# Three of eight wide weight splits in part two of the seven-product blocks done as two single splits

## The chip, the cores and the metric

The kernel runs on one core of one Trainium2 chip. The metric is the device time of one launch in microseconds (us), the median over runs. Matrix products run on TensorE (PE), elementwise work on VectorE (DVE) and ScalarE (ACT), some DMAs and a few operations on GpSimd (POOL), and most DMAs are issued from SyncE (SP).

## The reference, cut to what matters

One decoder layer over 512 tokens of width 2048: a norm, one wide input projection, two token mixers, and an output projection that is merged with gates.

```python
u = _rmsnorm(h, norm_w)
proj = jnp.matmul(u, w_in.astype(jnp.float32))
...
h_a = _mlstm_chunkwise(...)          # 8 heads
h_b = _gated_delta_chunkwise(...)    # 16 heads
y_a = jnp.matmul(h_a, w_out[:ML_WIDTH])
y_b = jnp.matmul(h_b, w_out[ML_WIDTH:])
return jax.nn.sigmoid(gate_a) * y_a + jax.nn.sigmoid(gate_b) * y_b
```

All of it is float32. The change concerns only how the weights of the large products are prepared.

## The kernel before, in words

**Products in three pieces.** A float32 product is made from three products of reduced-precision operands: each operand x becomes a pair, hi (a rounded copy) and lo (x minus hi), and the kernel adds hi·hi, hi·lo and lo·hi. For a weight tile, hi is a cast on ACT (`split_hi`, line 140) and lo a subtraction on DVE (`split_lo`, line 143) that has to wait for the cast. In the seven-product stages the three matmuls are lines 577, 578 and 579; line 578 is the one that reads lo.

**Seven products.** Most of the input projection and part of the output projection are done in blocks that save one of eight products of 2x2 sub-matrices: `seven_stage`, called once for the 13 blocks of `SEVEN` (kinds z, z, z, z, s, s, q, v, v, g, g, g, g) and once for the 2 blocks of `OUTS` (kind y). The function `seven` runs one block. A block has two parts, A and B, and each part has eight *quads*, here called A0 to A7 and B0 to B7. A quad loads three 128x512 weight pieces (`load_quad`, line 505) and makes weight pairs from them:

- A quad of part A makes two sums (lines 519 and 520), splits one sum and one raw piece singly, and splits the other two sums, `t13`, as one 128x1024 pair. It makes four products.
- A quad of part B makes one difference `ts` (line 537, from a raw piece and a piece that part A wrote to DRAM), splits it singly, and splits its other two raw pieces as one 128x1024 pair. It makes three products, the pair's two first and that of `ts` last.

Each product is made for two halves of the tokens, three matmuls a half, so that a quad of part B issues 18 matmuls.

**Buffers.** Single splits go into the tags `wh` and `wl` of the pool `wp`, with four buffers each. Wide splits go into `w2h` and `w2l`, with two buffers each. The raw pieces lie in `wr3` with three buffers.

**Between the parts.** When the last quad of part A is done, the eight PSUM banks hold sums that part B adds to. So as each half of a product of A7 ends, the bank is added into the SBUF tile X: `copy1` (line 562, ACT) twice for the first product, and `add` (line 631, DVE) six times, in the order m1, m1, m5, m5, m7, m7. The products of B0 write m1, m5 and m7 again, each in two halves, and each half has to wait until its bank's add has read it. The last of the six adds therefore stands ahead of the sixth group of three matmuls of B0.

**What sets the order.** `prep_sums` and `prep_pair` prepare quad n+1 while quad n is multiplied. TensorE keeps the order in which the code is written. On all other engines a scheduler sets the order when the kernel is built, by priorities (`tc.high_priority`) and its own estimate of when operands are ready; on the chip each engine then goes through its list in that order.

The lines that the change touches are in `prep_pair`:

Of the kernel before, what the change touches and what calls it, by code (L numbers as in the profile page):

```python
# [30 lines left out]
KH = KT // 2  # L31
# [27 lines left out]
def hybrid_body(  # L59
# [79 lines left out]
    def split_hi(hi, src):  # L139
        newest["A"] = A.copy(hi, src).ins  # L140

    def split_lo(lo, src, hi):
        newest["V"] = V.tensor_tensor(out=lo, in0=src, in1=hi.bitcast(F32), op=ALU.subtract).ins  # L143
# [336 lines left out]
    def seven_stage(sbp, su, s4, X, t2_d, w_, k0, blocks, sinks, hook, queue):  # L480
# [4 lines left out]
        quads = [(kind, c1, c2, b, g, i) for b, (kind, c1, c2) in enumerate(blocks)  # L485
                 for g in "AB" for i in range(KH)]
# [20 lines left out]
        def split(src, wide):  # L507
            if wide:
                hi, lo = (sbp.tile([P, 2, NO], F32R, tag=f"w2{n}", name=f"w{n}", bufs=2) for n in "hl")
            else:  # L510
                hi, lo = (wp.tile([P, 1, NO], F32R, tag=f"w{n}", name=f"w{n}", bufs=NSPL) for n in "hl")
            split_hi(hi, src)
            split_lo(lo, src, hi)
            return [(hi[:, n, :], lo[:, n, :]) for n in range(2 if wide else 1)]
# [25 lines left out]
        def prep_pair(q):  # L540
            if q < len(quads):
                p_, pair = partq[q]
                with tc.high_priority(offset=2 * PRIO):
                    w2 = split(pair, True)
                partq[q] = p_ + w2 if quads[q][4] == "A" else w2 + p_

        JW, OO = ((psj, "pj"), (psw, "wk")), ((pso, "o"),) * 2
# [16 lines left out]
        def seven(n0, kind, c1, c2):  # L564
# [20 lines left out]
            for n in range(N - 2):  # L585
                prep_sums(n0 + n + 1)
                prep_pair(n0 + n + 1)
                load_quad()
                for m in range(4 if n < KH else 3):
                    if n == N - 3 and m == 2:  # L590
                        prep_sums(n0 + N - 1)
                        prep_pair(n0 + N - 1)
                    product(n, m)
# [3 lines left out]
            for n, m in ((N - 2, 0), (N - 2, 1), (N - 1, 0), (N - 1, 1), (N - 2, 2), (N - 1, 2)):  # L597
                if (n, m) == (N - 2, 1):
                    prep_sums(n0 + N)
                if (n, m) == (N - 1, 0):  # L600
                    prep_pair(n0 + N)
                    load_quad()
                if last and (n, m) == (N - 1, 1):
                    hook()
                product(n, m)
# [1159 lines left out]
```

## Time and profile before

| | us |
|---|---|
| median of 3 runs | 2178.43 (2174.1 to 2181.12) |
| the profiled execution | 2172.99 |
| its span, first to last instruction | 2171.2 |
| PE busy | 2131.3 |
| DVE busy | 1715.0 |
| ACT busy | 1035.5 |
| granted TensorE clock, mean | 0.999 |

The profile lists a matmul of 512 columns with about 0.39 us, but the next one starts 0.23 us after it: matmuls overlap in the array, so a pause of PE shows as idle time only from 0.16 us on. DVE and ACT overlap likewise at their ends by about 0.09 us. Of the 13 blocks of `SEVEN` the first starts at about 124 us and the last ends at about 1130 us; the 2 blocks of `OUTS` lie between about 1957 and 2118 us.

### The profile page before, as it was taken

What the parts mean: (1) busy time and instruction counts of PE and PEld (TensorE: products, weight loads), DVE (VectorE), ACT (ScalarE), POOL (GpSimd) and SP (SyncE); (2) the same over time, 40 slices, a digit from 0 to 9 for tenths busy, and PEclk for the clock granted to TensorE, in tenths of its full rate; (3) what the DMA queues carried; (4) which work ended last, traced back from release to release, by engine and by line L of the source; (5) the groups of instructions that cost most, each with busy time, mean ns of one, the idle gap of its engine ahead of it and who ended that gap; (6) DMA issues with size and microseconds to landing.
All of it is one profiled execution on the core that took longest, in us unless ns stands there. A gap on an engine that the chain in (4) does not pass through costs nothing. (4 is left out here: it accounts for less than half of the span.)

```text
span 2171.2 us, 31926 instructions
## 1 busy us (share of the span) xinstructions
PE 2131.3 (98%) x10544; PEld 1756.0 (81%) x10544; DVE 1715.0 (79%) x2973; ACT 1035.5 (48%) x1994; POOL 432.0 (20%) x651
## 2 busy tenths in 40 slices
PE   6999999999999999999999999999999999999998
PEld 5888888888788887878878888888888888887786
DVE  5887788788788778777866887887887878668877
ACT  5444444444444444444445546456455464435345
POOL 0000000000004000000003335234243263243211
PEclk9999999999999999999999999999999999999999
DMA  5456676667668766766766767677686677778886
GB/s 160 124 185 202 195 213 199 213 199 226 198 222 245 242 191 219 242 186 222 257 197 172 196 173 184 169 181 185 178 222 171 165 185 209 198 239 266 232 281 242
DMA packets 447143, 444.20 MB, mean 205 GB/s; under 512 B 197121, under 2 KB 303842, under 8 KB 446850
## 3 DMA queue, kind: packets, MB, share of 16 engines
q1 hardware_dynamic: 377618, 337.22, 54.1%
q0 software_dynamic: 24752, 72.90, 10.8%
q10 hardware_dynamic: 44608, 32.06, 4.6%
q8 instruction: 82, 1.34, 0.3%
q14 instruction: 83, 0.68, 0.1%
HBM read 348.66 MB, written 97.58 MB: 206 GB/s over the span
## 5 line engine op out<-in xcount | busy, mean ns | idle before, releaser
L140 ACT CAST wh<-wr 128x512 fp32r<-128x512 f32 (+1 forms) x522 | 373.2, 717 | 415.4 <-PE pj L258 231.4
L143 DVE TENSOR_TENSOR wl<-wr,wh 128x512 fp32r<-128x512 f32 (+1 forms) x522 | 437.4, 840 | 109.3 <-ACT wh L140 103.7
L257 PE MATMUL pj<-uh,wh 128*128 128x512 f32 x896 | 376.0, 420 | 0.0
L259 PE MATMUL pj<-uh,wl 128*128 128x512 f32 x896 | 350.8, 391 | 0.0
L258 PE MATMUL pj<-ul,wh 128*128 128x512 f32 x896 | 350.2, 391 | 0.0
L578 PE MATMUL ps<-wl,uh 128*128 128x512 f32 x752 | 295.0, 392 | 4.8 <-DVE wl L143 4.8
L577 PE MATMUL ps<-wh,uh 128*128 128x512 f32 x752 | 294.5, 392 | 4.1 <-DVE X L631 3.5
L579 PE MATMUL ps<-wh,ul 128*128 128x512 f32 x752 | 292.8, 389 | 0.0
L140 ACT CAST wh<-ts 128x512 fp32r<-128x512 f32 x240 | 148.2, 617 | 250.9 <-DVE ts L537 197.8
L140 ACT CAST wh<-t 128x1024 fp32r<-128x1024 f32 x120 | 126.4, 1054 | 275.7 <-PE ps L579 165.7
L577 PE MATMUL ps<-wh,suh 128*128 128x512 f32 x624 | 242.9, 389 | 1.5 <-ACT to L642 1.5
L533 POOL DMA_DIRECT2D t_d<-ts x104 | 56.6, 544 | 936.9 <-DVE ts L520 883.0
L578 PE MATMUL ps<-wl,suh 128*128 128x512 f32 x624 | 242.8, 389 | 0.0
L579 PE MATMUL ps<-wh,sul 128*128 128x512 f32 x624 | 242.7, 389 | 0.0
L259 PEld LDWEIGHTS pj<-uh,wl 128*128 128x128 f32 x896 | 168.3, 188 | 37.3
L257 PEld LDWEIGHTS pj<-uh,wh 128*128 128x128 f32 x896 | 169.0, 189 | 30.0
L258 PEld LDWEIGHTS pj<-ul,wh 128*128 128x128 f32 x896 | 169.2, 189 | 28.1
L143 DVE TENSOR_TENSOR wl<-ts,wh 128x512 fp32r<-128x512 f32 x240 | 163.7, 685 | 35.2 <-ACT wh L140 35.2
L143 DVE TENSOR_TENSOR wl<-t,wh 128x1024 fp32r<-128x1024 f32 x120 | 146.8, 1224 | 55.9 <-ACT wh L140 55.0
L578 PEld LDWEIGHTS ps<-wl,uh 128*128 128x128 f32 x752 | 141.1, 188 | 40.7 <-DVE wl L143 12.7
L577 PEld LDWEIGHTS ps<-wh,uh 128*128 128x128 f32 x752 | 141.1, 188 | 40.1 <-DVE X L631 10.8
L537 DVE TENSOR_TENSOR ts<-wr 128x512 f32<-128x512 f32 x120 | 82.8, 690 | 104.2 <-DMA wr<-t_d 86.1
(334 smaller groups left out, 3826.2 us busy)
## 6 DMA issues: line engine op xcount, KB each, us to landing
wr<-in_w_in_dram SPq DMA_DIRECT2D x744, 256.0 KB, 3.8
wr<-in_w_out_dram SPq DMA_DIRECT2D x138, 256.0 KB, 5.0
t_d<-ts POOLq DMA_DIRECT2D x104, 256.0 KB, 3.9
wr<-t_d SPq DMA_DIRECT2D x104, 256.0 KB, 3.9
xt<-in_x_dram SPq DMA_DIRECT2D x8, 512.0 KB, 7.1
tg_d<-X ACTq DMA_DIRECT2D x16, 256.0 KB, 6.9
tg_d<-to ACTq DMA_DIRECT2D x16, 256.0 KB, 6.0
v<-v_d SPq DMA_DIRECT2D x8, 512.0 KB, 5.8
```

The source lines that it names most:

```text
L140: newest["A"] = A.copy(hi, src).ins
L143: newest["V"] = V.tensor_tensor(out=lo, in0=src, in1=hi.bitcast(F32), op=ALU.subtract).ins
L257: T.matmul(ps[j], hi[:, k, wsl], uh[:, kt, :], start=(kt == 0), stop=False)
L258: T.matmul(ps[j], hi[:, k, wsl], ul[:, kt, :], start=False, stop=False)
L259: T.matmul(ps[j], lo[:, k, wsl], uh[:, kt, :], start=False, stop=(kt == KT - 1))
L533: queue.dma_start(t2_d[b % 2, i], ts[:, 0, :])
L537: V.tensor_tensor(out=ts[:, 0, :], in0=r[:, 0, :], in1=r[:, 2, :], op=ALU.subtract)
L577: T.matmul(ps[t], ah, hi, start=(g == "A" and i == 0), stop=False, skip_group_check=True)
L578: T.matmul(ps[t], ah, lo, start=False, stop=False, skip_group_check=True)
L579: T.matmul(ps[t], al, hi, start=False, stop=(i == KH - 1), skip_group_check=True)
```

## The change

In part B, the quads B1, B3 and B5 (i odd and below 7) no longer split their pair of raw pieces into one 128x1024 buffer of `w2h` and one of `w2l`, but each piece by itself into a 128x512 buffer of `wh` and of `wl`. B0, B2, B4, B6 and B7, and all of part A, stay as they were. Three quads in each of 15 blocks are touched: 45 wide casts and 45 wide subtractions become 90 and 90 of half the size. Products, their order on TensorE and all values stay the same.

```diff
         def prep_pair(q):
             if q < len(quads):
                 p_, pair = partq[q]
+                _, _, _, _, g, i = quads[q]
                 with tc.high_priority(offset=2 * PRIO):
-                    w2 = split(pair, True)
+                    if g == "B" and i % 2 and i < KH - 1:
+                        w2 = split(pair[:, 0:1, :], False) + split(pair[:, 1:2, :], False)
+                    else:
+                        w2 = split(pair, True)
                 partq[q] = p_ + w2 if quads[q][4] == "A" else w2 + p_
```

The new lines move what stands below them by four: line 577 becomes 581, line 578 becomes 582, line 631 becomes 635, line 562 becomes 566.

The scheduler also orders the work around them anew. On DVE at the passage from part A to part B of the seventh block (kind q), before; `wr_5422` holds the raw pieces of B0, `wr_5467` of B1, `wr_5505` of B2, `wr_5551` of B3, `wr_5583` of B4:

```order
L143 TENSOR_TENSOR wl<-wr_5422,wh 128x1024
L631 TENSOR_TENSOR X<-X,ps 128x512
L537 TENSOR_TENSOR ts<-wr_5505 128x512
L631 TENSOR_TENSOR X<-X,ps 128x512 x3
L143 TENSOR_TENSOR wl<-ts,wh 128x512
L631 TENSOR_TENSOR X<-X,ps 128x512 x2
L537 TENSOR_TENSOR ts<-wr_5551 128x512
L143 TENSOR_TENSOR wl<-wr_5467,wh 128x1024
L143 TENSOR_TENSOR wl<-wr_5505,wh 128x1024
L143 TENSOR_TENSOR wl<-ts,wh 128x512
L537 TENSOR_TENSOR ts<-wr_5583 128x512
```

And now, where the pieces of B0 to B4 are `wr_5494`, `wr_5539`, `wr_5577`, `wr_5627` and `wr_5659`:

```order
L143 TENSOR_TENSOR wl<-wr_5494,wh 128x1024
L635 TENSOR_TENSOR X<-X,ps 128x512
L537 TENSOR_TENSOR ts<-wr_5577 128x512
L143 TENSOR_TENSOR wl<-wr_5539,wh 128x512
L635 TENSOR_TENSOR X<-X,ps 128x512 x2
L143 TENSOR_TENSOR wl<-wr_5539,wh 128x512
L635 TENSOR_TENSOR X<-X,ps 128x512 x2
L537 TENSOR_TENSOR ts<-wr_5627 128x512
L143 TENSOR_TENSOR wl<-wr_5577,wh 128x1024
L635 TENSOR_TENSOR X<-X,ps 128x512
L537 TENSOR_TENSOR ts<-wr_5659 128x512
```

The lo halves of B1 have moved ahead of adds, as two single ones, and the last add now stands behind the difference of B3 and the wide lo half of B2. In the other blocks the rows differ a little, but in every one the last add has come to stand behind the wide lo half of B2.

On ACT at the same place, before:

```order
L140 CAST wh<-wr_5422 128x1024
L562 COPY X<-ps 128x512 x2
L140 CAST wh<-ts 128x512
L140 CAST wh<-wr_5467 128x1024
L140 CAST wh<-wr_5505 128x1024
L140 CAST wh<-ts 128x512
L140 CAST wh<-wr_5551 128x1024
L140 CAST wh<-ts 128x512 x2
L140 CAST wh<-wr_5583 128x1024
```

And now:

```order
L140 CAST wh<-wr_5494 128x1024
L566 COPY X<-ps 128x512 x2
L140 CAST wh<-wr_5539 128x512 x2
L140 CAST wh<-wr_5577 128x1024
L140 CAST wh<-wr_5659 128x1024
L140 CAST wh<-ts 128x512 x2
L140 CAST wh<-wr_5627 128x512 x2
L140 CAST wh<-wr_5727 128x1024
L140 CAST wh<-ts 128x512 x2
```

The casts of B1's pieces now come right behind the two copies, the wide cast of B4 has moved ahead of the casts of two differences, and B3's two pieces come behind those. On TensorE no row has moved. On SP one load of a mixer's values and two loads of the output projection stand a few places elsewhere in the whole program, and on POOL one load has changed places with its neighbours.

## The prediction, before the run

> **What bounds the kernel now.** First the page: how full is each engine, and what ends the pauses of the fullest.
>
> ```profile
> span 2171.2 us, 31926 instructions
> PE 2131.3 (98%) x10544; PEld 1756.0 (81%) x10544; DVE 1715.0 (79%) x2973; ACT 1035.5 (48%) x1994; POOL 432.0 (20%) x651
> ```
>
> PE lacks 40 us to the span, so whatever the change saves on DVE or ACT is worth nothing unless PE waits for it, and all that it can take off is among PE's pauses. The view of waits lists them for PE: us in total, times, the longest.
>
> ```profile
> PE pprm L108 <- POOL rs L304: 14.6, 1, 14.6
> PE ps L578 <- DVE wl L143: 5.2, 12, 0.9
> PE ps L577 <- DVE X L631: 3.5, 6, 1.4
> ```
>
> 14.6 us are the start. In the 15 blocks PE waits 12 times for a lo half, 5.2 us, and 6 times for an add into X, 3.5 us. Since a pause shows only beyond 0.16 us (0.39 us of a matmul less its spacing of 0.23), the true losses are 12 x 0.16 = 1.9 and 6 x 0.16 = 1.0 us larger. The first kind is what the change aims at.
>
> The place is the passage from part A to part B. PE in the seventh block, in order of time; 632.24 is the first matmul of B0, and a matmul follows each 0.23 us:
>
> ```profile
> 632.24 0.39 PE L577 MATMUL ps<-wh,uh 128*128 128x512 f32 x1
> ...
> 636.19 0.39 PE L577 MATMUL ps<-wh,uh 128*128 128x512 f32 x1
> ...
> 636.88 0.39 PE L577 MATMUL ps<-wh,uh 128*128 128x512 f32 x1
> 637.73 0.50 PE L578 MATMUL ps<-wl,uh 128*128 128x512 f32 x1 [0.45 <-DVE wl L143]
> ```
>
> 636.19 is the last half of B0's third product, which needs the sixth add. 636.88 is B1's first matmul. The second, which reads lo, comes 0.85 us after it, 0.62 late. DVE at the same time:
>
> ```profile
> 628.10 1.22 DVE L143 TENSOR_TENSOR wl<-wr,wh 128x1024 fp32r<-128x1024 f32 x1
> 629.24 0.68 DVE L631 TENSOR_TENSOR X<-X,ps 128x512 f32<-128x512 f32 x1
> 631.65 0.69 DVE L537 TENSOR_TENSOR ts<-wr 128x512 f32<-128x512 f32 x1 [1.73 <-DMA wr<-t_d]
> 632.26 1.88 DVE L631 TENSOR_TENSOR X<-X,ps 128x512 f32<-128x512 f32 x3
> 634.05 0.69 DVE L143 TENSOR_TENSOR wl<-ts,wh 128x512 fp32r<-128x512 f32 x1
> 634.65 1.28 DVE L631 TENSOR_TENSOR X<-X,ps 128x512 f32<-128x512 f32 x2
> 635.85 0.69 DVE L537 TENSOR_TENSOR ts<-wr 128x512 f32<-128x512 f32 x1
> 636.45 2.35 DVE L143 TENSOR_TENSOR wl<-wr,wh 128x1024 fp32r<-128x1024 f32 x2
> ```
>
> DVE runs without a gap from 631.65 on: it is the bound here, because B2's difference stood in its list ahead of five adds and waited 1.73 us for its transfer. Spacings are read here too: 0.60 us from one 512-wide operation to the next (632.26 to 634.05 for three), and 2.35 - 1.22 = 1.13 us from one wide one to the next. B1's wide lo ended at 636.45 + 1.22 = 637.67, and PE went on 0.06 later.
>
> **The change part by part.** *B1's lo halves.* Two single ones now stand ahead of adds, so the wait at B1 goes: 0.62 us in this block. *The sixth add.* In the new list it stands behind two halves of B1, B3's difference and B2's wide lo; before, only one half of a difference stood there. DVE takes its list in order: at 631.65 B2's difference sat waiting while the adds behind it did not start. So I walk the new list from that row with the spacings above: difference of B2 631.65, half 632.26, adds two and three 632.86 and 633.46, half 634.06, adds four and five 634.66 and 635.26, difference of B3 635.86, wide lo of B2 636.47, sixth add 637.60 to 638.28. PE's last half of the third product then starts at 638.34 instead of 636.19, 2.15 us later. What was waited for at B1 comes back (0.62): this block loses **1.53 us**.
>
> Do the two halves get their casts in time? ACT there:
>
> ```profile
> 627.97 1.07 ACT L562 COPY X<-ps 128x512 f32<-128x512 f32 x2
> 632.43 0.62 ACT L140 CAST wh<-ts 128x512 fp32r<-128x512 f32 x1 [3.40 <-DVE ts L537]
> 632.96 1.05 ACT L140 CAST wh<-wr 128x1024 fp32r<-128x1024 f32 x1
> ```
>
> ACT idles 3.40 us after the copies, and two casts of 0.62 fit before 632.26. The wide cast at 632.96 was B1's, in the buffer that A7 had left; that buffer now falls to B2, whose cast can end at about 634, well before 636.47.
>
> The block is not special. The ninth block had no wait at B1 and no late transfer to speak of:
>
> ```profile
> 782.90 0.68 DVE L631 TENSOR_TENSOR X<-X,ps 128x512 f32<-128x512 f32 x1
> 783.96 0.69 DVE L537 TENSOR_TENSOR ts<-wr 128x512 f32<-128x512 f32 x1 [0.38 <-DMA wr<-t_d]
> ...
> 789.31 0.39 PE L577 MATMUL ps<-wh,uh 128*128 128x512 f32 x1
> ...
> 789.99 0.39 PE L577 MATMUL ps<-wh,uh 128*128 128x512 f32 x1
> 790.22 0.39 PE L578 MATMUL ps<-wl,uh 128*128 128x512 f32 x1
> ```
>
> The same walk from 783.96 (5.95 us to the start of the sixth add) has it at 789.91 to 790.59 and PE at 790.65 instead of 789.31: a loss of **1.34**, and nothing to get back. In the second block, as in the next three, B3's difference stood ahead of the sixth add already, and waited for its transfer:
>
> ```profile
> 247.44 0.69 DVE L537 TENSOR_TENSOR ts<-wr 128x512 f32<-128x512 f32 x1 [0.31 <-DMA wr<-t_d]
> 248.05 0.68 DVE L631 TENSOR_TENSOR X<-X,ps 128x512 f32<-128x512 f32 x1
> 248.79 0.51 PE L577 MATMUL ps<-wh,uh 128*128 128x512 f32 x1 [0.54 <-DVE X L631]
> 249.60 0.40 PE L577 MATMUL ps<-wh,uh 128*128 128x512 f32 x1
> 249.92 0.51 PE L578 MATMUL ps<-wl,uh 128*128 128x512 f32 x1
> ```
>
> 248.05 is the sixth add. Now the fifth takes its place, the wide lo follows at 248.65, the sixth add runs from 249.78 to 250.46, and PE starts at 250.52 instead of 248.79: 1.73 later, less 0.1 for B1's lo, which came 0.32 after its predecessor: **1.6**. The three walks give 1.3 to 1.6; over 15 blocks at 1.5 that is **+22 us**.
>
> *Later quads.* B4 and B6 no longer share two wide buffers with B1, B3 and B5, so their casts can start earlier. The lo waits that are not at B1 can go: between nothing and the whole 5.2 + 1.9 us of the view of waits. Part of it lies at B1 and is in the walks already, so I take less than half, **-3 us**.
>
> *More instructions.* 45 wide casts and subtractions become 90 and 90 single ones.
>
> ```profile
> L143 DVE TENSOR_TENSOR wl<-wr,wh 128x512 fp32r<-128x512 f32 x402 | 291.7, 726 | 91.8 <-ACT wh L140 86.2 <-PE put L313 2.2 <-DMA wr<-in_w_out_dram 1.2
> L143 DVE TENSOR_TENSOR wl<-wr,wh 128x1024 fp32r<-128x1024 f32 x120 | 145.9, 1222 | 17.6 <-ACT wh L140 17.5
> L140 ACT CAST wh<-wr 128x512 fp32r<-128x512 f32 x402 | 247.4, 617 | 325.2 <-PE pj L258 231.4 <-PE py L1389 41.0 <-issue 13.5
> L140 ACT CAST wh<-wr 128x1024 fp32r<-128x1024 f32 x120 | 126.0, 1051 | 90.2 <-PE ps L579 71.5 <-issue 13.6 <-ACT wh L140 4.9
> 589.00:666.00 77.00, 76.48 (x336) 62.40 (x335) 64.16 (x83) 34.09 (x51) 7.68 (x14) 1.00 0.68 216
> ```
>
> By busy time ACT gains 45 x (2 x 0.617 - 1.051) = 8.2 us and DVE 45 x (2 x 0.726 - 1.222) = 10 us; by spacing, which counts in a queue without gaps, DVE gains 45 x (2 x 0.60 - 1.13) = 3.2 us. In the last row (a stretch of one block; PE, weight loads, DVE, ACT busy) DVE has 13 us to spare and ACT 43, so outside the passage I count them at nothing; without that cover they cost those 3 to 10 us. In the passage the walk has them already.
>
> [...]
>
> *Moved transfers.* One load of a mixer's values, two of the output projection (SP) and one on POOL move by a few places, each of 256 KB to 512 KB.
>
> ```profile
> wr<-in_w_out_dram SPq DMA_DIRECT2D x138, 256.0 KB, 5.0
> ```
>
> They are issued several transfers ahead; I take zero, and bound it by one landing each, 4 x 5 = 20 us at worst, nothing at best. B4's pieces can be loaded earlier, since B1's are read sooner.
>
> The sum: 22 - 3 = +19 us on the profiled execution's 2172.99 us gives 2192. The median of the runs shown is 5.4 us above that execution, which would give 2197. I put the prediction between: **2195 us**.
>
> **The rivals.** *No change (2178 us).* The sixth add cannot start earlier than its list allows: in the ninth block B0 began at 789.31 - 15 x 0.227 = 785.91, the first add 3.01 us before it, and from there to the sixth nine operations and the first take 0.60 + 5.95 us, so it ends 4.2 us after B0's first matmul, and PE needs it at 3.40. Even without any wait for a transfer a block loses 0.9 us, 13 in all; set against that everything PE waited before (5.2 + 3.5 + 2.9 = 11.6 us), the change comes out even. It needs the transfers of B2 to be on time in all blocks, and nothing in the change moves them: in the row of 631.65 the wait was 1.73 us.
>
> *Faster (2171 us).* It is decided by one point: whether the sixth add ends within 3.40 us of B0's first matmul. If it does (it would, were B2's wide lo, 1.13 us, behind it), the waits for lo halves go and nothing takes their place: -7 us. For it speaks that B1's lo is indeed ready early; against it, the list, and three walks with 1.3 us and more beyond that point.
>
> *Slower still (2210 us).* B3's and B5's halves need single buffers that the products of B1 and B3 hold, and their casts stand behind those of two differences in ACT's list. If each of these two quads waits 0.5 us for its lo half, that is 15 x 2 x 0.5 = 15 us more. A quad lasts 18 x 0.23 = 4.1 us and a cast with its lo 1.3, so the slack is there unless a transfer is late; the page's wait for `t_d` shows that some are.
>
> *The clock falls (2257 us).* If the longer pauses made the throttle grant half speed for one quad per block, 15 x 4.1 = 62 us would come on top. The longest pause in these stages says no:
>
> ```profile
> 821.75 0.39 PE L579 MATMUL ps<-wh,sul 128*128 128x512 f32 x1
> 823.59 0.50 PE L577 MATMUL ps<-wh,suh 128*128 128x512 f32 x1 [1.45 <-ACT to L642]
> 823.93 0.40 PE L578 MATMUL ps<-wl,suh 128*128 128x512 f32 x1
> 824.16 0.39 PE L579 MATMUL ps<-wh,sul 128*128 128x512 f32 x1
> ```
>
> After 1.84 us between two starts the spacing is back at 0.23 with the third matmul. [...]
>
> **How the numbers follow.** About 0.3% (6.5 us) is what a measurement of this kernel can tell from no change. Forecast, the late sixth add: 0.75, 2195 us, by itself 2187 to 2203. Slower still: 0.10. The clock: 0.01. No change: 0.09. Faster: 0.05. So slower by over 0.3%: 0.85 (0.01 of the forecast's chance falls within the bound instead), within: 0.10, faster: 0.05. The range reaches from 2184, into the no-change case, to 2207, into the slower one; outside lie faster, most of no change and half of slower still, not quite 0.2.
>
> **What would show it.** In the new profile: PE's waits for an add into X grow from 3.5 to 20 us or more, at the third product of B0, and those for a lo half shrink below 2 us. DVE's rows at the passage have the sixth add behind a 128x1024 lo. PE's busy time stays within some us of 2131 while the span grows. If PE waits at B3 or B5 instead, the third rival holds; if the sixth add is in time, the walk's spacings were wrong.

## The result and the profile after

| | before | after |
|---|---|---|
| median of 6 runs, us | 2180.66 (2174.1 to 2184.57) | 2193.91 (2192.01 to 2197.74) |
| ratio, 95% interval | | 1.0065 [1.0047, 1.0083] |
| profiled execution, us | 2172.99 | 2193.82 |
| its span, us | 2171.2 | 2192.1 |

The change makes the kernel slower by 0.65%, 13 us by the medians and 21 by the two profiled executions; that of before lay 7.7 us under its median, that of after at its median. What before's slower executions wait for is only in part on record (its second profile, below). The page of after, span and busy times:

```profile
span 2192.1 us, 31988 instructions
PE 2134.5 (97%) x10544; PEld 1756.7 (80%) x10544; DVE 1711.6 (78%) x3018; ACT 1047.3 (48%) x2039; POOL 431.2 (20%) x651
```

No engine has become the bound: PE is busy 3 us longer in a span that is 21 us longer, DVE 3 us less although it has 45 instructions more. What grew is PE's waiting. The view of waits for PE (us in total, times, the longest):

```profile
PE ps L581 <- DVE X L635: 22.3, 29, 1.3
PE pprm L108 <- POOL rs L304: 15.2, 1, 15.2
PE ps L582 <- DVE wl L143: 5.0, 5, 3.0
```

The wait for an add into X was 3.5 us in 6 times and is 22.3 in 29. That for a lo half has hardly changed in sum (5.2 to 5.0), but comes 5 times in place of 12.

The passage of the seventh block, first DVE from the first add to the sixth, then PE from B0's first matmul to the sixth group:

```profile
637.53 0.68 DVE L635 TENSOR_TENSOR X<-X,ps 128x512 f32<-128x512 f32 x1
639.66 0.69 DVE L537 TENSOR_TENSOR ts<-wr 128x512 f32<-128x512 f32 x1 [1.45 <-DMA wr<-t_d]
640.27 0.68 DVE L143 TENSOR_TENSOR wl<-wr,wh 128x512 fp32r<-128x512 f32 x1
640.87 1.28 DVE L635 TENSOR_TENSOR X<-X,ps 128x512 f32<-128x512 f32 x2
642.07 0.69 DVE L143 TENSOR_TENSOR wl<-wr,wh 128x512 fp32r<-128x512 f32 x1
642.67 1.28 DVE L635 TENSOR_TENSOR X<-X,ps 128x512 f32<-128x512 f32 x2
643.86 0.69 DVE L537 TENSOR_TENSOR ts<-wr 128x512 f32<-128x512 f32 x1
644.47 1.22 DVE L143 TENSOR_TENSOR wl<-wr,wh 128x1024 fp32r<-128x1024 f32 x1
645.60 0.68 DVE L635 TENSOR_TENSOR X<-X,ps 128x512 f32<-128x512 f32 x1
```

```profile
640.54 0.39 PE L581 MATMUL ps<-wh,uh 128*128 128x512 f32 x1
...
644.66 0.39 PE L583 MATMUL ps<-wh,ul 128*128 128x512 f32 x1
646.34 0.50 PE L581 MATMUL ps<-wh,uh 128*128 128x512 f32 x1 [1.28 <-DVE X L635]
```

The sixth add starts 5.94 us after B2's difference; the walk in the prediction had 5.95. It ends at 646.28, and PE's sixth group starts at 646.34. Without a pause matmuls of 512 columns follow one another at 0.227 us (before, 700.19 to 711.98: 52 spacings in 11.79 us), so that group would start 15 x 0.227 = 3.40 us after B0's first matmul; it starts 5.80 after it, against 3.95 before. There is no pause any more at B1.

One sum serves all kernels below. For each product matmul of the 15 blocks I take from the trace its start less that of the one before it less 0.227 us, and add up what is over 0.015 us: **at the passage** (the 18 matmuls of B0 and the first 4 of B1) and **elsewhere**. Before has 14.5 and 8.1 us, after 33.5 and 9.8: 20.7 more, and the span is 20.9 longer. So the whole loss between these two executions is in these pauses, 19.0 us of it at the passage. There the sixth group of three matmuls has 20.0 us against 2.4 before, the five groups ahead of it 13.5 against 6.4 (the adds two to five have the halves of B1 ahead of them), and B1 nothing against 5.8.

### The profile page after: what moved, and what is told of

It reads as the page before. It is cut to its first block, busy times and chain, and to the rows that moved or that the text cites. A ratio compares the mean times of both kernels' runs of the same rounds, so it can differ in the third digit from the quotient of the medians.

```text
span 2192.1 us, 31988 instructions
## 1 busy us (share of the span) xinstructions
PE 2134.5 (97%) x10544; PEld 1756.7 (80%) x10544; DVE 1711.6 (78%) x3018; ACT 1047.3 (48%) x2039; POOL 431.2 (20%) x651
## 3 DMA queue, kind: packets, MB, share of 16 engines
q8 instruction: 82, 1.34, 0.3%
## 5 line engine op out<-in xcount | busy, mean ns | idle before, releaser
L140 ACT CAST wh<-wr 128x512 fp32r<-128x512 f32 (+1 forms) x567 | 381.9, 676 | 552.4 <-PE pj L258 237.8
L143 DVE TENSOR_TENSOR wl<-wr,wh 128x512 fp32r<-128x512 f32 (+1 forms) x567 | 442.6, 783 | 109.8 <-ACT wh L140 104.7
L581 PE MATMUL ps<-wh,uh 128*128 128x512 f32 x752 | 296.5, 394 | 20.5 <-DVE X L635 20.1
L582 PE MATMUL ps<-wl,uh 128*128 128x512 f32 x752 | 294.0, 391 | 4.5 <-DVE wl L143 4.5
L583 PE MATMUL ps<-wh,ul 128*128 128x512 f32 x752 | 293.5, 390 | 0.0
L582 PE MATMUL ps<-wl,suh 128*128 128x512 f32 x624 | 242.8, 389 | 0.0
L583 PE MATMUL ps<-wh,sul 128*128 128x512 f32 x624 | 242.7, 389 | 0.0
L582 PEld LDWEIGHTS ps<-wl,uh 128*128 128x128 f32 x752 | 141.5, 188 | 34.0 <-DVE wl L143 5.7
```

The source lines that it names most:

```text
L581: T.matmul(ps[t], ah, hi, start=(g == "A" and i == 0), stop=False, skip_group_check=True)
L582: T.matmul(ps[t], ah, lo, start=False, stop=False, skip_group_check=True)
L583: T.matmul(ps[t], al, hi, start=False, stop=(i == KH - 1), skip_group_check=True)
```

## The experiments

`issue_after(i)` tells the scheduler to put an instruction behind `i`; both are on DVE here, and the moved row follows at the usual spacing (below, the wide lo 0.60 us after the add, at 637.25 and 636.65). All kernels but the last two in this table were timed in 5 rounds beside runs of before; a second profile of after and of before is in brackets.

| kernel | median, us | ratio to before, 95% | span | at the passage | elsewhere |
|---|---|---|---|---|---|
| only B1 split | 2194.39 | 1.0061 [1.0044, 1.0078] | 2193.7 | 39.4 | 3.8 |
| only B3 and B5 split | 2176.11 | 0.9976 [0.9964, 0.9987] | 2178.7 | 15.7 | 12.3 |
| not split in kind y | 2192.90 | 1.0051 [1.0036, 1.0067] | 2190.5 | 31.3 | 9.6 |
| B2's wide lo behind the sixth add | 2172.11 | 0.9958 [0.9944, 0.9972] | 2171.4 | 20.5 | 2.6 |
| and B3's difference | 2169.11 | 0.9961 [0.9945, 0.9976] | 2165.3 | 13.3 | 3.8 |
| and B2's difference | 2157.49 | 0.9903 [0.9888, 0.9919] | 2156.4 | 2.0 | 6.0 |
| the same, only B3 and B5 split | 2163.26 | 0.9927 [0.9912, 0.9942] | 2157.9 | 3.6 | 5.1 |
| before, B2's difference behind the sixth add | 2168.21 | 0.9952 [0.9934, 0.9970] | 2165.5 | 6.4 | 11.0 |
| after (again) | 2193.91 | 1.0065 [1.0047, 1.0083] | 2192.1 (2195.1) | 33.5 (36.7) | 9.8 (9.8) |
| before (again) | 2180.66 | | 2171.2 (2176.0) | 14.5 (15.5) | 8.1 (10.4) |

The kernel with the best median has only four runs. In all twelve profiles the span less the two sums lies between 2148.1 and 2150.7 us, whatever was split and in whatever order. That is the strongest reading of the study: to within 2.6 us no other part of the program gained or lost.

### Which of the three quads carries the loss

Only B1 split:

```diff
-                    if g == "B" and i % 2 and i < KH - 1:
+                    if g == "B" and i == 1:
```

> Only B1 is split into two single buffers; B3 and B5 stay wide as before. Theory (the sixth add is late because B1's freed wide buffer lets B2's wide lo and two halves stand ahead of it): the rows on DVE at the passage are those of the changed kernel, so its pauses at the passage stay (33 us over 15 blocks against 15 before), and the fourteenth block's new waits for lo halves of B3 and B5 with the fall of the clock (5.0 us) go: 2189 us, range 2186 to 2192. Rival (the price lies in the 90 more instructions on each of ACT and DVE): a third of the instructions, a third of the 13 us: 2185 or less. Rival (B3 and B5 carry it): 2181.

Measured 2194.39 us, as much as with all three. PE's waits:

```profile
PE ps L581 <- DVE X L635: 25.9, 26, 4.0
```

Waits for a lo half in the blocks are gone from the list, those for an add are all that is left. Both rivals fall: 15 of 45 pairs bring the whole loss. The time is 5 us above what I expected and outside my range: in the profile the waits at B3 and B5 went, but another came, 4.0 us in the fifteenth block, for an add behind B2's difference, which waited 3.64 us for its transfer.

Only B3 and B5 split:

```diff
-                    if g == "B" and i % 2 and i < KH - 1:
+                    if g == "B" and i in (3, 5):
```

> Only B3 and B5 are split singly; B1 stays wide. Theory: the sixth add stands where it stood before, behind one half of a difference (and B3's difference in four blocks), so the passage costs 15 us of pauses as before, not 33; in the fourteenth block B3 and B5 may wait for their halves as in the changed kernel: 2176 us with that wait, 2171 without it, range 2170 to 2182. Rival (more instructions): two thirds of the 13 us stay, 2189. Rival (transfers moved elsewhere in the program make the loss): 2190 or more.

Measured 2176.11, the theory's figure, and faster than before by 0.24% [0.13, 0.36]. The passage is that of before:

```profile
PE ps L582 <- DVE wl L143: 8.2, 14, 1.6
PE ps L581 <- DVE X L635: 4.6, 8, 1.2
```

Thirty split pairs cost nothing that can be measured.

### Is it the place of the sixth add

All 45 pairs split, one order more. `newest["add"]` is the add issued last, at this place the sixth:

```diff
-            split_lo(lo, src, hi)
+            with tc.issue_after(after) if after is not None else ExitStack():
+                split_lo(lo, src, hi)
...
-                        w2 = split(pair, True)
+                        w2 = split(pair, True, newest["add"] if g == "B" and i == 2 else None)
```

> The changed kernel with one order more: B2's wide lo is issued on DVE behind the sixth add (in all 15 blocks). Nothing is left out, all 45 pairs stay split. Theory: the sixth add ends 1.13 us sooner, so the pause at the sixth group of B0 shrinks from 1.4 to 0.3 us in nine blocks and goes in the six with 0.8 to 0.9: 9 x 1.13 + 5 x 1.04 + 0.9 = 16 us less, 2178 us, range 2173 to 2182. Rival (more instructions, or the transfers): it stays within 3 us of the changed kernel's 2194. Rival (a new wait takes its place, B2's lo): PE then waits at B2 in most blocks and the time stays above 2188.

Measured 2172.11: 22 us under the changed kernel and 9 under before, with the same 90 small casts and subtractions. PE's waits:

```profile
PE ps L582 <- DVE X L636: 10.6, 13, 3.2
```

(L582 is here the first product, L636 the add and L538 the difference.) DVE in the seventh block, where B0's first matmul is at 633.17:

```profile
636.04 0.69 DVE L538 TENSOR_TENSOR ts<-wr 128x512 f32<-128x512 f32 x1
636.65 0.68 DVE L636 TENSOR_TENSOR X<-X,ps 128x512 f32<-128x512 f32 x1
637.25 1.22 DVE L143 TENSOR_TENSOR wl<-wr,wh 128x1024 fp32r<-128x1024 f32 x1
```

The sixth add now stands ahead of the wide lo, and PE's sixth group starts 4.21 us after B0's first matmul instead of 5.80. The order alone takes the loss away; the rivals "more instructions" and "transfers" are excluded (by the names in the two traces, the order on SP differs from that of the changed kernel in one load only). It is 6 us better than the theory, and 1 below its range. The pauses at the sixth group fell from 20.0 to 3.6 us, the 16 that I expected; the passage as a whole fell by 13.0, since a late transfer made an add of the fifteenth block 3.4 us late. The pauses elsewhere fell by 7.2 us, 6.3 of them in the fourteenth block; why this order helps there is not shown.

Then B3's difference behind the sixth add as well:

```diff
-                    V.tensor_tensor(out=ts[:, 0, :], in0=r[:, 0, :], in1=r[:, 2, :], op=ALU.subtract)
+                    with tc.issue_after(newest["add"]) if i == 3 else ExitStack():
+                        V.tensor_tensor(out=ts[:, 0, :], in0=r[:, 0, :], in1=r[:, 2, :], op=ALU.subtract)
```

> As the kernel with B2's wide lo behind the sixth add, and B3's difference behind it as well. Theory (each 512-wide row of DVE ahead of the sixth add costs its spacing of 0.60 us as long as that add is late): the pause of 0.30 us, with the 0.11 of its follower, that is left at the sixth group of B0 in nine blocks goes: 9 x 0.41 = 3.7 us less than 2172, 2168 us, range 2165 to 2172. Rival (the remaining lateness is set by B2's difference, which waits for its transfer with the adds behind it, and nothing else matters): 2172, no change.

Measured 2169.11, 3.0 us less by the medians, but its ratio to before is the same, so the time decides nothing. The profile does: the pause at the sixth group of B0, 0.3 us in nine blocks (0.15 in one of them), is in none of them any more. The passage is now at 13.3 us, under the 14.5 of before, with all pairs still split.

And B2's difference too (`i in (2, 3)` in place of `i == 3`):

> All 45 pairs split as in the changed kernel; on DVE B2's difference, B3's difference and B2's wide lo are issued behind the sixth add. Theory (what is left of the pauses at the passage, 20.5 us in the profile of the kernel with only the wide lo behind the add, are adds that stand behind B2's difference while that waits for its transfer): they go, and 2.6 us elsewhere stay: 2172 - 20 = 2152 us, range 2149 to 2162. Rival (the wait moves to B2's own products, since its difference and its lo come later): 2165 or more, with waits for a lo half at the groups of B2.

Measured 2157.49, 1% faster than before and inside the range, 5 us above the 2152 of the sum. DVE at the passage of the seventh block (B0's first matmul at 626.30):

```profile
623.29 0.68 DVE L637 TENSOR_TENSOR X<-X,ps 128x512 f32<-128x512 f32 x1
623.88 0.69 DVE L143 TENSOR_TENSOR wl<-wr,wh 128x512 fp32r<-128x512 f32 x1
624.49 1.28 DVE L637 TENSOR_TENSOR X<-X,ps 128x512 f32<-128x512 f32 x2
625.68 0.68 DVE L143 TENSOR_TENSOR wl<-wr,wh 128x512 fp32r<-128x512 f32 x1
626.28 1.87 DVE L637 TENSOR_TENSOR X<-X,ps 128x512 f32<-128x512 f32 x3
628.08 1.28 DVE L539 TENSOR_TENSOR ts<-wr 128x512 f32<-128x512 f32 x2
```

```profile
PE ps L584 <- DVE wl L143: 1.4, 3, 0.8
PE ps L583 <- DVE X L637: 0.6, 2, 0.4
```

(L583, L584 and L637 are here the first product, the second and the add.) DVE no longer waits for a transfer between the adds. The sixth ends at 628.15, 1.85 us after B0's start and 1.55 ahead of its need; B2's difference, moved behind it, finds its transfer landed. Of 33.5 us at the passage 2.0 are left. This is the fastest kernel of the study.

### What the split is worth once the adds are in time

Before, with nothing split, and only B2's difference moved behind the sixth add:

```diff
-                    V.tensor_tensor(out=ts[:, 0, :], in0=r[:, 0, :], in1=r[:, 2, :], op=ALU.subtract)
+                    with tc.issue_after(newest["add"]) if i == 2 else ExitStack():
+                        V.tensor_tensor(out=ts[:, 0, :], in0=r[:, 0, :], in1=r[:, 2, :], op=ALU.subtract)
```

> The kernel before, nothing split, but B2's difference issued on DVE behind the sixth add. Theory (the sixth add's place and time set the passage, split or not): of the 14.5 us of pauses at the passage in the profile of before most go, the 8.1 us elsewhere stay: 2180.6 - 13 = 2168 us, range 2162 to 2173. Rival (B1's wide lo, now behind two differences that wait for transfers, becomes late): PE waits for lo halves at B1 in most blocks, 2176 or more.

Measured 2168.21, as forecast. No wait for an add is left in the blocks, but those for lo halves have grown:

```profile
PE ps L579 <- DVE wl L143: 9.5, 13, 1.4
```

In five blocks PE is late at B1 by 0.5 to 1.6 us each: its wide lo now stands behind two differences, and where one of these waits for a transfer, B1 does too. That is the rival's mechanism, in too few blocks for the rival's time. (L578 and L579 are here the first and the second product.)

With the order of the fastest kernel, but only B3 and B5 split:

> Only B3 and B5 split singly, and B2's difference, B3's difference and B2's wide lo issued on DVE behind the sixth add. Theory (with the adds first the passage costs nothing either way, and splitting B1 is worth only its own lo waits): within 4 us of the kernel with all three split and the same order, 2152 to 2158. Rival (B1's wide lo is late again behind the two differences): 0.5 us per block more, 2160 or more.

Measured 2163.26, 5 us above the theory's end and in the rival's range. Its profile shows the pause at B1's lo again in the third, fifth, thirteenth and fourteenth block, 0.2 to 1.0 us each. So with the adds first, splitting B3 and B5 is worth 4.9 us (2168.21 to 2163.26) and splitting B1 another 5.8 (to 2157.49). Each step alone is near the width of the intervals; both together, 10.7 us, are well outside it (0.9952 [0.9934, 0.9970] against 0.9903 [0.9888, 0.9919]). In all three kernels the six adds stand ahead of the differences of B2 and B3 in every block, so the steps compare like with like. Whether B1's wide lo, unsplit but issued ahead of these two differences, would do as well was not tried; it is a rival to the 5.8 us.

### The fourteenth block

After has 11.8 us of pauses in this block, before 6.8. The rows of DVE and of PE in after:

```profile
2036.06 0.69 DVE L537 TENSOR_TENSOR ts<-wr 128x512 f32<-128x512 f32 x1 [4.28 <-DMA wr<-t2o_d]
2036.67 0.68 DVE L143 TENSOR_TENSOR wl<-wr,wh 128x512 fp32r<-128x512 f32 x1
...
2045.54 0.69 DVE L537 TENSOR_TENSOR ts<-wr 128x512 f32<-128x512 f32 x1 [5.85 <-DMA wr<-t2o_d]
2046.15 0.69 DVE L143 TENSOR_TENSOR wl<-ts,wh 128x512 fp32r<-128x512 f32 x1
2046.75 1.29 DVE L143 TENSOR_TENSOR wl<-wr,wh 128x512 fp32r<-128x512 f32 x2
```

```profile
2037.40 0.50 PE L582 MATMUL ps<-wl,uh 128*128 128x512 f32 x1 [1.13 <-DVE wl L143]
...
2044.11 0.39 PE L581 MATMUL ps<-wh,uh 128*128 128x512 f32 x1
2047.49 0.50 PE L582 MATMUL ps<-wl,uh 128*128 128x512 f32 x1 [2.99 <-DVE wl L143]
```

The single lo halves of B3 and B5 stand behind a later quad's difference, which waits 4.28 and 5.85 us for its piece; PE waits for them 1.3 and 3.15 us beyond its spacing. To see whether the split does this, the two blocks of kind y were left wide:

```diff
-                    if g == "B" and i % 2 and i < KH - 1:
+                    if g == "B" and i % 2 and i < KH - 1 and quads[q][0] != "y":
```

> The changed kernel, but the two blocks of the output projection (kind y, the fourteenth and fifteenth) keep the wide pair in all quads. Theory: the fourteenth block loses its waits of 1.3 and 3.15 us for halves of B3 and B5 and the half-speed clock behind the second; these two blocks take again 6.8 and 1.05 us of pauses instead of 11.8 and 1.6: 5.5 us less, 2188 us, range 2186 to 2191; no granted clock of 0.5 in the stage. Rival (those waits are a late transfer of this one execution and not the split): 2193 to 2195.

Measured 2192.90, outside the theory's range and 1.0 us under the changed kernel, with intervals that overlap. The waits at B3 and B5 are gone from its profile, but the fourteenth block has one of 2.3 us for a lo half of B6, its granted clock fell to 0.50 at another place (1982.17 to 1985.58), and it has 8.1 us of pauses where 6.8 were expected. So I took a second profile of each kernel.

> The changed kernel once more, for a second profile. Open: whether the waits of 1.3 and 3.15 us for halves of B3 and B5 in the fourteenth block belong to the split or to one execution's late transfers. Theory (late transfers): the pauses at the passage, 33.5 us in the first profile, come again within 3 us, block by block at the same groups, and those of the fourteenth block's B3 and B5 do not come again at the same size. Rival (the split): B3 and B5 of the fourteenth block wait again for 1 us or more each.

DVE and PE in the second profile of after:

```profile
2038.84 0.69 DVE L537 TENSOR_TENSOR ts<-wr 128x512 f32<-128x512 f32 x1 [4.05 <-DMA wr<-t2o_d]
...
2047.62 0.69 DVE L537 TENSOR_TENSOR ts<-wr 128x512 f32<-128x512 f32 x1 [5.14 <-DMA wr<-t2o_d]
```

```profile
2040.19 0.50 PE L582 MATMUL ps<-wl,uh 128*128 128x512 f32 x1 [0.96 <-DVE wl L143]
2049.57 0.50 PE L582 MATMUL ps<-wl,uh 128*128 128x512 f32 x1 [2.28 <-DVE wl L143]
```

Both waits come again, at the same quads: beyond its spacing PE is 1.1 and 2.4 us late, against 1.3 and 3.15. So they belong to the changed kernel and not to one execution. The passage comes again too, with 36.7 us against 33.5, a little more than the 3 us allowed. But the waits are not the doing of the split of B3 and B5 alone: with only these two split, the fourteenth block has one such pause, 1.4 us at B5, and 6.25 us in all; and in the three kernels that have all 45 pairs split and B2's wide lo behind the sixth add, neither wait is there.

> The kernel before once more, for a second profile; the first lay 7.7 us below the median of 2180.7. Expected: the passage again at 14.5 us of pauses within 3 us, and what makes an execution slower than the first one lies at the groups that wait for late transfers (lo halves of the last quads, the fourteenth and fifteenth block).

Before's second profile (span 2176.0) has 15.5 us at the passage; its fifteenth block waits 4.6 us for an add, behind a difference that waited 4.62 us for its transfer. That place alone has 5.8 us more than in the first profile, in a block that was named beforehand; the waits of the last quads changed little. But the passages of the other fourteen blocks have 8.7 us against 13.5, so that the two sums agree by luck: the passage of before varies by some us from one execution to the next. In kind y late transfers of `t2o_d` make PE wait with and without the split; the split and the order change where. What the split costs in the fourteenth block by itself stays open: the kernel not split in kind y gains 1.0 us by the medians and has 3.7 us less of pauses there, and the two pairs of profiles of before and after differ there by 5.0 and 4.0.

## Why the prediction was right, point by point

- **The time.** Forecast 2195, measured 2193.91; the sum on the profiled execution gave 2192, and that of after took 2193.82. The mechanism forecast is the one that the profiles and the runs show. That the figure is so close is partly luck: two errors of the sum nearly cancel (below), and by the medians the loss is 13.3 us where 16.6 was forecast (2195 less 2178.43).
- **The sixth add, +22 us.** Right in kind, a little large. The list was walked to 0.01 us, from the row of B2's difference on. In the seventh block the loss was 1.22 us against 1.53 forecast, since that difference's transfer came 0.29 us sooner after B0's start; in the ninth it was 1.60 against 1.34, in the second 1.24 against 1.6. Over 15 blocks the passage costs 19.0 us more, 1.27 a block against 1.5. That the place in the list is the cause is shown: the same kernel with only B2's wide lo behind the add is 22 us faster, and its pauses at the sixth group are 16.5 us smaller.
- **B1's lo wait goes.** Right: no pause at B1 in any block. Its price lay in the walks.
- **Later quads, -3 us.** This step was wrong. The pauses elsewhere rose by 1.7 us (8.1 to 9.8). In the 13 blocks of `SEVEN` the waits at B6 did go, but the fourteenth block brought the mechanism of the rival "slower still", a split quad's half behind a late transfer, in force in one block where the rival had it in all. So one sign named beforehand failed: PE's waits for lo halves did not shrink below 2 us but are 5.0, of which 4.1 are at B3 and B5 of that block. The term was off by 4.7 us, and the first one by 3.0 the other way; the errors nearly cancel in the sum (+19 forecast, +20.7 in the pauses).
- **More instructions, 0.** Right. ACT's busy time grew by 11.8 us (8.2 forecast). The DVE rows of the raw pieces' lo halves, after:

```profile
L143 DVE TENSOR_TENSOR wl<-wr,wh 128x512 fp32r<-128x512 f32 x492 | 351.5, 717 | 97.6 <-ACT wh L140 92.6 <-PE put L313 2.2 <-DMA wr<-in_w_out_dram 0.7
L143 DVE TENSOR_TENSOR wl<-wr,wh 128x1024 fp32r<-128x1024 f32 x75 | 91.5, 1220 | 12.3 <-ACT wh L140 12.0
```

  Together 443.0 us, against 437.6 before: 5.4 more, between the 3.2 of spacing and the 10 of busy time. None of it shows in the span: the span less the pauses is the same with and without the split, and with all pairs split and the adds first the kernel runs 1% faster than before.
- **Moved transfers, 0 (at worst 20).** Span less pauses is the same to 2.6 us in all twelve profiles, so nothing of the 20 us appeared outside the pauses. Undoing the moves alone was not tried.
- **The clock, 0.01.** Not the 62 us of the rival, but the argument against it was too confident: see the last section. The pause that it took for the longest, 1.61 us beyond the spacing, was not quite that: the fourteenth block had one of 1.65.
- **No change.** This rival needed B2's transfers to be on time. In the seventh block B2's difference still waited 1.45 us, with adds behind it; and the ninth lost 1.60 us where the rival had 0.9.

## What to carry to other kernels

A freed buffer lets a scheduler issue its consumer sooner, and since DVE went through its list in order here (in the second profile of before an add behind a difference that waited 4.62 us for its transfer kept PE waiting 4.6 us) that moves everything behind it, here the one add on which the next PSUM group waits; so walk the new list with the spacings of the trace (here 0.60 us for a 512-wide row and 1.13 for a 1024-wide one) before counting the saved wait. That B1's freed wide buffer is what let B2's wide lo move up is read from the new order; no run gave the wide splits a third buffer to show it. What empties PSUM for the next products belongs ahead of preparation for later ones, and an operation that waits for a transfer should not stand ahead of either (22 us for the wide lo and 11.6 for B2's difference, 2169.11 to 2157.49, by the medians here). With that order put right the same split was worth about 11 us here, so a change that loses may be sound and only badly placed.

## What the runs showed of the hardware that was not expected

The granted clock fell to 0.50 in short stretches, which none of the blocks in the first profile of before had (1.00 from 124 to 1130 us and from 1957 to 2118). The change seems not to be needed for them: in the second profile of before PE starts again at 2090.24, behind a pause of 4.8 us, and its next matmuls follow one another at 0.43 us (2090.84, 2091.27, 2091.69) in place of 0.23, as those of after do in its stretch at 0.50. The stretches of after around its 3.15 us pause (us; busy us and instructions of PE, weight loads, DVE, ACT, POOL; granted clock; DMA share; GB/s):

```profile
2047.40:2048.90 1.50, 1.41 (x6) 1.19 (x7) 1.50 (x3) 0.00 (x0) 0.00 (x0) 1.00 0.44 142
2048.91:2052.32 3.41, 3.41 (x10) 2.63 (x9) 3.38 (x6) 1.24 (x2) 0.54 (x1) 0.50 0.82 285
```

The fall came 1.4 us after PE had started again, lasted 3.41 us and cost 8 matmuls 0.2 us each, 1.6 us. The pause need not be that long: in the fastest kernel a pause of 1.66 us ended at 1950.52, with 0.3 us of smaller ones just before, and the clock fell to 0.50 too, 0.84 us later:

```profile
1947.94:1951.35 3.41, 1.90 (x8) 1.19 (x8) 3.41 (x7) 1.14 (x2) 3.41 (x6) 1.00 1.03 224
1951.36:1954.77 3.41, 3.41 (x10) 2.63 (x9) 3.41 (x6) 2.32 (x3) 2.02 (x4) 0.50 1.07 264
```

At the same place of before PE starts again at 1964.00, behind a pause of 1.65 us and 0.3 us of smaller ones, and the clock stayed at 1.00 (1958.00 to 1967.10, and on to 2118). In the kernel with B2's wide lo behind the add a pause of 3.36 us ended at 2087.70, and the clock was still at 1.00 for the 2.07 us that the second row shows after it:

```profile
2082.94:2086.35 3.41, 1.56 (x7) 0.94 (x6) 0.58 (x1) 1.04 (x1) 0.00 (x0) 1.00 0.97 366
2086.36:2089.77 3.41, 2.07 (x9) 1.74 (x10) 3.41 (x5) 0.00 (x0) 0.00 (x0) 1.00 1.00 384
```

So the length of a pause does not tell by itself: the clock fell after 1.66 us in one kernel and stayed after 1.65 at the same place of another. The prediction's argument, one pause of 1.61 us after which the spacing was back at 0.23, is therefore not enough to say that the pauses of the changed kernel leave the clock alone; in after it fell, behind 3.15 us. What tells the cases apart is not shown; no run was made for it.
